# A head's two keys projected with the pairs, kept raw in DRAM, and prepared beside its queries

## The chip, the cores and the metric

The kernel runs on one core of a Trainium2 chip. The metric is the device time of one execution in microseconds (us); the time before is the median of three runs, 2295.79 us (2294.99 to 2299.85).

## The reference, cut to what matters

One step of a two-layer trunk over 512 latent ("sample") and 128 context ("prompt") tokens, 640 columns here. The odd layer projects its normed input with one matrix and splits the columns; mixer C is differential attention over four heads, each with two queries, two keys and a value of twice the width.

```python
cq, ck, cv, cg, dq, dk, dv, dg = split_cols(h @ w_in, ODD_SPLIT)
cq, ck = rms_norm(cq, cqn), rms_norm(ck, ckn)        # per head, 128 wide
# sample tokens: rope on cq and ck; cached context keys and values joined ahead
o1 = attend(cq[:, 0], ck_all[:, 0], cv_all)
o2 = attend(cq[:, 1], ck_all[:, 1], cv_all)
o_c = rms_norm(o1 - lam * o2, c_on) * (1.0 - lam_init)
y_c = o_c * silu(cg)
```

The prompt tokens' normed keys are an output too (`new_c_k`).

## The kernel before, in words

Activations lie transposed, features on partitions, in 16 tiles `h` of 128 x 640, each as a high and a low fp32r part; products are formed from three matmuls (high x high, high x low, low x high). A tile of 128 output columns is made from 16 weight blocks. The weights come in quarters of four blocks (256 KB, `load_raw`, on SP's queue), which ACT and VectorE split into `wh` and `wl` (lines 220 and 221, four buffers each); a quarter is 24 matmuls, two halves of 320 columns.

The odd projection has four stages.

1. Six gate tiles (`FRONT[:6]`), projected directly.
2. `run_pairs` (line 444): the rest of `FRONT`, 16 tiles of values and gates, two at a time. A pair is computed as one 2 x 2 block product in seven products of 24 matmuls (`Q1 N5 P6 Q2 P7 Q3 P4`, lines 535 to 537) from sums of weight halves, which VectorE makes, and sums of `h` halves, made before. The two results go to `kept` tiles (lines 1384 to 1399) and to DRAM on POOL's queue (line 1362): values raw to `vdram`, gates to `ydram`. During N5 the first halves of `h[0..7]` hold other data; behind the last pair's P7 they are read back from `hdram` (line 1404).
3. `run_tiles` (line 317, called at 1570) with attention beside it. The first three jobs, query 0, query 1 and key 0 of head 3, are **leads**: they go through the weights together, quarter by quarter, with three PSUM pairs. Then one tile per job, each quarter's matmuls followed by `slot()` (line 308), which advances every generator in `prep` by one step; `proj_parts` advances attention five times per tile. The leads' preparations are begun one behind the other during and right behind job 3 (`settle`, line 378).
4. The output projection.

Preparing a key (`k_gen`, line 578): the projected tile is staged in SBUF, transposed to rows on TensorE (`to_rows`, line 560: four 128 x 128 blocks of the sample and one of the prompt, each group into one of the two PSUM buffers `T`), squared and summed on ACT (line 589, five squares), multiplied by the gain on VectorE (591, 594), scaled by the root from POOL (596 to 598), rotated (605 to 609), and, some steps later, transposed back and split into `k0h`, `k0l` (613 to 622). The context's cached key goes the same way through `ctxk`. Preparing a query (`q_gen`, 627): `qx` and `qsq` on ACT (631, 632), four copies `qsw` (635), three VectorE operations (636 to 639), then sums of squares by TensorE into a `T` buffer (643) and transposes of those (651). The values are read from `vdram` (`v_load`, 693) and laid out by `v_kept` (698), which puts the head's attention into `attn`. `scores` (741), `soft` (712) and `diff_gen` (1437) are the attention.

A scheduler fixes each engine's order when the program is built; every engine then runs its list in order.

Of the kernel before, what the change touches and what calls it, by code (L numbers as in the profile page):

```python
# [11 lines left out]
F32 = mybir.dt.float32  # L12
# [8 lines left out]
P = 128  # L21
# [4 lines left out]
NT = NS + NP  # L26
# [14 lines left out]
P_BUFS = 4  # L41
# [9 lines left out]
def trunk_kernel(ctx: ExitStack, tc: tile.TileContext, I: dict, O: dict):  # L51
    nc = tc.nc
# [17 lines left out]
    pools = {}  # L70
# [212 lines left out]

    prep, attn = [], []

# [31 lines left out]
    def run_tiles(jobs, w_ap, make_h, fill=None, rate=0.0, ahead=None, order=(0, 1, 2, 3), before=None,  # L317
                  last=None, by_half=False, mid=False, trans=[], grace=0, cut=None, summed=None, led=None, freed=None):
# [13 lines left out]
        units = [(pos, qd, js) for pos, qd in enumerate(order) for js in (cut or [(0, 4)])]  # L332
        for ui, (pos, qd, js) in enumerate(units):
# [64 lines left out]
        t = 0  # L398
        if before:
            settle()  # L400
        else:
            n = pending.pop(0)
            begin(jobs[n][1], pps[n])
# [173 lines left out]

    def k_gen(ap, pp, tag, src, gain, new_out, then=None, more=0):
# [20 lines left out]
        nc.gpsimd.dma_start(new_out, kg[:, 4, :])  # L599
        m1 = ap.tile([P, 4, P], F32, tag="rp", name="m1", bufs=3)  # L600
        m2 = ap.tile([P, 4, P], F32, tag="rp", name="m2", bufs=3)
        x = kg[:, 0:4, :].rearrange("p b (a h f) -> p (b a) h f", a=2, h=2)
# [244 lines left out]
    xdram = [dram.tile([P, NT], F32, name=f"xd{k}") for k in range(KT)]  # L847
    vdram = [dram.tile([P, NT], F32, name=f"vd{k}") for k in range(10)]
    hdram = [dram.tile([P, 2, HALF], F32R, name=f"hd{k}") for k in range(8)]

# [480 lines left out]
    def forms1():  # L1331
# [3 lines left out]
        for j, tag in enumerate((3, 4, 5, 6, 7, 1, 2, 0)):  # L1335
# [7 lines left out]
            if j in (4, 6):  # L1343
# [9 lines left out]
    def front_col(kind, i):  # L1353
        return (OD["cv"] + i * P if i < 8 else OD["dv"] + (i - 8) * P) if kind == "v" else \
            (OD["cg"] + i * P if i < 8 else OD["dg"] + (i - 8) * P)
# [4 lines left out]
    def keep_tile(n):  # L1360
        kind, i = FRONT[n]
        nc.gpsimd.dma_start((vdram if kind == "v" else ydram)[i], st["kept", n])

# [188 lines left out]
    heads = (3, 0, 1, 2)  # L1552
    for n, h in enumerate(heads):
        load, vgen = v_then(256, I["cache_c_v"][0, 0, h], (2 * h, 2 * h + 1), O["new_c_v"][0, 0, h], diff_then(n, h))
        for m in range(2):
            jobs.append((OD["cq"] + (m * 4 + h) * P, q_job(f"q{m}" + "ab"[n % 2], "c_q_norm")))
        for m in range(2):
            job = k_job(f"k{m}", I["cache_c_k"][0, 0, m, h], "c_k_norm", O["new_c_k"][0, 0, m, h], *((vgen, 1 - min(n, 1)) if m else (None, 1)))
            jobs.append((OD["ck"] + (m * 4 + h) * P, job if m else with_load(load, job)))
# [110 lines left out]
```

## Time and profile before

| | |
|---|---|
| median of three runs | 2295.79 us |
| the profiled execution | 2294.4 us, span 2292.6 us |
| TensorE busy | 2255.9 us |
| VectorE, ACT, POOL busy | 1589.8, 1088.9, 160.0 us |
| pairs ahead of attention | 1220.8 to 1417.8 us |
| first plain matmul behind them | 1417.8 us |
| granted TensorE clock | 0.999 |

The busy time of an engine is the union of its instructions' times. Matmuls overlap by design of the record, so the pace of TensorE is read from the distance between starts. A gap on TensorE has its own mark in the timeline: the idle time in brackets and what ended it.

### The profile page before, as it was taken

How to read it: one execution, taken by the hardware profiler on the slowest of the kernel's cores; microseconds unless marked ns; L12 is line 12 of the kernel's file. 1: busy time of each engine (PE TensorE's matmuls, PEld its weight loads, DVE VectorE, ACT ScalarE, POOL GpSimd, SP SyncE). 2: the span in 40 equal slices, each digit the busy share in tenths (PEclk: the TensorE clock that was granted, in tenths of full speed). 3: DMA queues.
4: the chain of work that ended last, by engine and by line, in shares of the span. 5: the costliest groups of instructions: out<-in, count | busy, mean ns of one | idle time of the engine just before them, and what ended most of it. 6: DMA issues, size and time to landing. Idle time of an engine off the chain costs nothing.

```text
span 2292.6 us, 41100 instructions
## 1 busy us (share of the span) xinstructions
PE 2255.9 (98%) x15900; PEld 2178.0 (95%) x15900; DVE 1589.8 (69%) x2831; ACT 1088.9 (47%) x2304; POOL 160.0 (7%) x224
## 2 busy tenths in 40 slices
PE   7999999999999999999999999999999999999999
PEld 5889999999999999999999999999999999999999
DVE  4666968779779776887787665365665655557775
ACT  5325652443522222544464443465565676755443
POOL 1001000000000000000100001011111100000101
PEclk9999999999999999999999999999999999999999
DMA  9985537547367564854553335223223221238642
GB/s 321 294 270 161 158 113 218 152 133 219 116 210 216 177 191 137 277 173 140 164 155 108 116 118 152 79 60 104 79 63 101 71 60 49 76 101 269 184 138 62
DMA packets 380899, 342.89 MB, mean 150 GB/s; under 512 B 16402, under 2 KB 338416, under 8 KB 380192
## 3 DMA queue, kind: packets, MB, share of 16 engines
q1 hardware_dynamic: 366288, 296.00, 43.0%
q0 software_dynamic: 13696, 42.10, 5.4%
q8 instruction: 125, 2.05, 0.4%
q10 hardware_dynamic: 720, 2.16, 0.3%
q14 instruction: 70, 0.57, 0.1%
HBM read 301.27 MB, written 38.93 MB: 148 GB/s over the span
## 4 chain that ended last, share of the span: by engine, by line
PE 85%; DVE 4%; ACT 4%; DMA 3%; issue 3%; POOL 1%; SPq 0%; ACTq 0%; POOLq 0%; DVEq 0%
PE pq L537 7%; PE pq L536 7%; PE pq L535 7%; PE pa L256 6%; PE pa L257 6%; PE pb L256 6%; PE pa L258 6%; PE pb L257 6%; PE pb L258 6%; PE pb L271 2%; PE pb L270 2%; PE pa L270 2%; PE pb L272 2%; PE pa L272 2%; PE pa L271 2%
## 5 line engine op out<-in xcount | busy, mean ns | idle before, releaser
L220 ACT ACTIVATE wh<-raw 128x512 fp32r<-128x512 f32 (+1 forms) x456 | 273.1, 600 | 574.0 <-PE pb L257 406.9
L221 DVE TENSOR_TENSOR wl<-raw,wh 128x512 fp32r<-128x512 f32 (+1 forms) x456 | 295.7, 650 | 212.3 <-ACT wh L220 191.9
L256 PE MATMUL pa<-h,wh 128*128 128x320 f32 x1024 | 325.3, 319 | 4.3 <-ACT h L220 2.0
L257 PE MATMUL pa<-h,wh 128*128 128x320 f32 x1024 | 319.5, 313 | 1.7 <-DVE h L221 0.8
L258 PE MATMUL pa<-h,wl 128*128 128x320 f32 x1024 | 318.2, 311 | 0.9 <-DVE wl L221 0.9
L257 PE MATMUL pb<-h,wh 128*128 128x320 f32 x1024 | 317.1, 310 | 0.0
L258 PE MATMUL pb<-h,wl 128*128 128x320 f32 x1024 | 316.8, 309 | 0.0
L256 PE MATMUL pb<-h,wh 128*128 128x320 f32 x1024 | 316.6, 310 | 0.0
L198 DVE SCALAR_TENSOR_TENSOR acc<-adaw,sT,acc 128x1024 f32<-128x1024 f32 x240 | 299.7, 1276 | 0.0
L256 PEld LDWEIGHTS pa<-h,wh 128*128 128x128 f32 x1024 | 193.1, 189 | 18.3 <-issue 10.0
L257 PEld LDWEIGHTS pa<-h,wh 128*128 128x128 f32 x1024 | 193.3, 189 | 7.6 <-issue 3.3
L535 PE MATMUL pq<-h,wh 128*128 128x320 f32 x640 | 198.7, 311 | 0.4 <-ACT wh L220 0.4
L537 PE MATMUL pq<-h,wl 128*128 128x320 f32 x640 | 198.0, 309 | 0.1
L536 PE MATMUL pq<-h,wh 128*128 128x320 f32 x640 | 197.7, 309 | 0.0
L258 PEld LDWEIGHTS pa<-h,wl 128*128 128x128 f32 x1024 | 193.1, 189 | 3.5 <-issue 2.1
L257 PEld LDWEIGHTS pb<-h,wh 128*128 128x128 f32 x1024 | 192.2, 188 | 1.0 <-issue 0.8
L256 PEld LDWEIGHTS pb<-h,wh 128*128 128x128 f32 x1024 | 192.1, 188 | 0.8 <-issue 0.4
L258 PEld LDWEIGHTS pb<-h,wl 128*128 128x128 f32 x1024 | 192.3, 188 | 0.0
L537 PE MATMUL pq<-T,wl 128*128 128x320 f32 x480 | 147.7, 308 | 0.2 <-DVE wl L221 0.2
L536 PE MATMUL pq<-T,wh 128*128 128x320 f32 x480 | 147.9, 308 | 0.0
L535 PE MATMUL pq<-T,wh 128*128 128x320 f32 x480 | 147.6, 308 | 0.1
L270 PE MATMUL pa<-h,wh 128*128 128x320 f32 x432 | 141.0, 326 | 0.0
(431 smaller groups left out, 5306.0 us busy)
## 6 DMA issues: line engine op xcount, KB each, us to landing
adaw<-in_ada_w SPq DMA_DIRECT2D x128, 512.0 KB, 4.3
raw<-in_ev_w_in SPq DMA_DIRECT2D x176, 256.0 KB, 3.5
raw<-in_od_w_in SPq DMA_DIRECT2D x160, 256.0 KB, 2.9
ada<-in_ada_w SPq DMA_DIRECT2D x32, 1024.0 KB, 7.9
w<-in_od_w_in SPq DMA_DIRECT2D x24, 512.0 KB, 4.0
yd<-y POOLq DMA_DIRECT2D x32, 320.0 KB, 3.2
yin<-yd SPq DMA_DIRECT2D x32, 320.0 KB, 4.5
w<-yd SPq DMA_DIRECT2D x32, 320.0 KB, 4.2
```

What stands on the lines that cost most here:

```text
L198: V.scalar_tensor_tensor(out=acc[c], in0=w, scalar=sT[:, kt, c:c + 1], in1=acc[c], op0=ALU.mult, op1=ALU.add)
L220: A.activation(hi, x, AF.Copy)
L221: V.tensor_sub(lo, x, hi)
L256: PE.matmul(ps, wh[:, i, :], hi[:, sl], start=(j == js[0] if alone else (pos == 0 and j == 0)), stop=False)
L257: PE.matmul(ps, wh[:, i, :], lo[:, sl], start=False, stop=False)
L258: last_mm[0] = PE.matmul(ps, wl[:, i, :], hi[:, sl], start=False, stop=(j == js[1] - 1 if alone else (pos == 3 and j == 3)))
L270: PE.matmul(ps, wh[:, j, :], hi[:, sl], start=(qd == 0 and j == 0), stop=False)
L271: PE.matmul(ps, wh[:, j, :], lo[:, sl], start=False, stop=False)
L272: PE.matmul(ps, wl[:, j, :], hi[:, sl], start=False, stop=(qd == 3 and j == 3))
L535: PE.matmul(ps, wh[:, j, :], hi, start=(new and h == 0 and j == 0), stop=False, **kw)
L536: PE.matmul(ps, wh[:, j, :], lo, start=False, stop=False, **kw)
L537: PE.matmul(ps, wl[:, j, :], hi, start=False, stop=(h == 1 and j == 3), **kw)
```

## The change

The two keys of head 3, the first differential head, are taken out of the jobs of stage 3 and put into `FRONT` as a ninth pair, tiles of kind `"r"`, behind the other heads' values and ahead of the last four value tiles. Like values they are kept raw, and go to two DRAM tiles `rdram`. `run_tiles` is called without leads (`n_lead=0`): query 0 and query 1 of head 3 are now plain jobs 0 and 1. Ahead of it `odd_start()` (the constants of the layer) and `first_head()` are called: the latter loads both raw keys into two of the attention's four `P` buffers, the value tile and its context, and puts a generator into a new list `early`, advanced once per `slot()` ahead of `prep`. After two idle steps it runs key 0's `k_gen`, key 1's and then the values' `v_kept`. These `k_gen`s read the raw tile where others stage theirs, and have their row tiles in the buffer of the value tile `vh` (`places`) instead of the three `rp` buffers.

```diff
     def slot(fill=None, rate=0.0, attend=True):
+        advance(early, len(early))
         advance(prep, len(prep))
...
-            leads, held, lp = list(range(min(3, len(jobs)))), [], None
+            leads, held, lp = list(range(n_lead)), [], None
...
-        x = stage(ap, pp)
+        x = stage(ap, pp) if places is None else pp
         yield
         ss = small.tile([P, 5], F32, tag="ss", name="ss")
-        kg = ap.tile([P, 5, P], F32, tag="rp", name="kg", bufs=3)
+        kg = place(0, 5, "kg")
...
-                                                for t in (("v", a), ("v", a + 1), ("g", b), ("g", b + 1))] +         [("v", i) for i in (4, 5, 8, 9)]
+                                                for t in (("v", a), ("v", a + 1), ("g", b), ("g", b + 1))] + \
+        [("r", i) for i in range(2)] + [("v", i) for i in (4, 5, 8, 9)]
...
+    FIRST = [OD["ck"] + (m * 4 + 3) * P for m in range(2)]
...
+    def first_head():
+
+        ap = pools["cur"]
+        raws = []
+        for i in range(2):
+            raws.append(ap.tile([P, 768], F32, tag="P", name="first", bufs=P_BUFS)[:, 0:NT])
+            nc.sync.dma_start(raws[-1], rdram[i])
+        load, vgen = c_then(0)
+        load()
+
+        def keys():
+            yield
+            yield
+            for m, x in enumerate(raws):
+                tag, src, gain, new_out = k_args(m, heads[0])
+                yield from k_gen(ap, x, tag, src, gains[gain], new_out, more=1,
+                                 places=ap.tile([P, 14, P], F32, tag="vh", name="kpl"))
+            yield from vgen()
+
+        early.append(keys())
...
-    run_tiles(jobs, I["od_w_in"][0], lambda k: odd_start() if k == 8 else None, mid=True)
+    odd_start()
+    first_head()
+    run_tiles(jobs, I["od_w_in"][0], None, mid=True, n_lead=0)
```

How the built program's rows stand now. On ACT, the first place is where key 0 of head 3 is squared. Before (`stg` is the staged key, `junk,ss` a square with its sum, `wh` a weight split):

```order
L646 COPY qs<-T 96x256
L557 COPY stg<-pa 128x320
L220 ACTIVATE wh<-raw 128x512
L557 COPY stg<-pb 128x320
L589 ACTIVATE junk,ss<-T 128x128 x5
L220 ACTIVATE k0h<-T 128x256
```

After (line 596 is the square, 637 `qx`, 638 `qsq` and 641 `qsw` of the first query):

```order
L220 ACTIVATE wh<-raw 128x512
L637 ACTIVATE qx<-pb,vec 128x320
L596 ACTIVATE junk,ss<-T 128x128
L638 ACTIVATE qsq<-pb 128x320
L596 ACTIVATE junk,ss<-T 128x128
L641 COPY qsw<-qx 32x512
L596 ACTIVATE junk,ss<-T 128x128
L641 COPY qsw<-qx 32x512
L596 ACTIVATE junk,ss<-T 128x128
L641 COPY qsw<-qx 32x512
L596 ACTIVATE junk,ss<-T 128x128
L641 COPY qsw<-qx 32x512
```

The staging copies are gone, and the five squares, which stood in one row, alternate with the first query's work. Key 1 and the second query stand in the same way.

On VectorE, at the same place, before (`kg` the gained and normed rows, `m` the rotated ones, `k0l` a split of the laid-out key):

```order
L591 TENSOR_TENSOR kg<-T,gain_rows 128x512
L594 TENSOR_TENSOR kg<-T,gain_rows 128x128
L596 TENSOR_SCALAR ss<-ss 128x5
L598 TENSOR_TENSOR kg<-kg,r 128x640
L221 TENSOR_TENSOR k0l<-T,k0h 128x256
L605 TENSOR_TENSOR m_16631<-kg,tables 128x512
L606 SCALAR_TENSOR_TENSOR m_16632<-kg,tables 128x8x32
L608 TENSOR_TENSOR m_16632<-kg,tables 128x8x32
L221 TENSOR_TENSOR wl<-raw,wh 128x512
L609 TENSOR_TENSOR m_16631<-m_16631,m_16632 128x512
```

After (`kpl` are the rows in the value's buffer, `qsw` and `qm` the query's):

```order
L598 TENSOR_TENSOR kpl<-T,gain_rows 128x512
L601 TENSOR_TENSOR kpl<-T,gain_rows 128x128
L603 TENSOR_SCALAR ss<-ss 128x5
L642 TENSOR_TENSOR qsw<-qsw,tables 128x512
L605 TENSOR_TENSOR kpl<-kpl,r 128x640
L645 TENSOR_TENSOR qm<-qm,qsw 128x512
L611 TENSOR_TENSOR kpl<-kpl,tables 128x512
L612 SCALAR_TENSOR_TENSOR kpl<-kpl,tables 128x8x32
L614 TENSOR_TENSOR kpl<-kpl,tables 128x8x32
L221 TENSOR_TENSOR wl<-raw,wh 128x512
L615 TENSOR_TENSOR kpl<-kpl 128x512
```

Two operations of the query have come into the key's chain, and the context's split has left it.

On SP's queue, behind the pairs' last weights, before:

```order
L233 DMA raw<-in_od_w_in 128x4x128 x8
L1415 DMA lam_16213<-in_c_lambda 128x512
L1427 DMA con<-in_c_out_norm 128x256
L233 DMA raw<-in_od_w_in 128x4x128
L695 DMA vraw<-vd_194 128x640
L669 DMA ctxv<-in_cache_c_v 128x2x256
L580 DMA ctxk<-in_cache_c_k 128x2x128
```

After (`first` are the raw keys):

```order
L233 DMA raw<-in_od_w_in 128x4x128 x8
L1427 DMA lam_16268<-in_c_lambda 128x512
L1439 DMA con<-in_c_out_norm 128x256
L1579 DMA first<-rd_198 128x640
L1579 DMA first<-rd_199 128x640
L701 DMA vraw<-vd_194 128x640
L675 DMA ctxv<-in_cache_c_v 128x2x256
L587 DMA ctxk<-in_cache_c_k 128x2x128
```

The two raw keys stand behind the constants, and one weight load has moved behind the whole group; the eight weight loads ahead are now the two query tiles' own.

On TensorE, counted in quarters of 24 plain matmuls from the last pair: key 0's first transposes stand behind 4 quarters, the first query's sums of squares (L649) 25 matmuls behind them, key 0's layout behind 7, key 1's two places behind 8 and 11, the value tiles' transposes 4 matmuls behind key 1's layout and 20 matmuls behind that, and the first scores behind 12.9. Before, the first scores stood behind 20.9. TensorE's list is 24 instructions shorter, all of them projection matmuls. From shortly behind the first scores, every engine's list is that of before.

More of the change, by code (lines that the diff above doesn't have):

```diff
@@ L331, in run_tiles @@
                else new_pp(1 + held.index(n) if trans else n) for n in leads}
-        units = [(pos, qd, js) for pos, qd in enumerate(order) for js in (cut or [(0, 4)])]
+        units = [(pos, qd, js) for pos, qd in enumerate(order) for js in (cut or [(0, 4)])] if leads else []
         for ui, (pos, qd, js) in enumerate(units):
@@ L400, in run_tiles @@
             settle()
-        else:
+        elif pending:
             n = pending.pop(0)
@@ L575, in gate, with k_gen, place @@
                                    op0=ALU.add, op1=ALU.mult)
-    def k_gen(ap, pp, tag, src, gain, new_out, then=None, more=0):
+    def k_gen(ap, pp, tag, src, gain, new_out, then=None, more=0, places=None):
+        def place(c, b, name):
+            if places is None:
+                return ap.tile([P, b, P], F32, tag="rp", name=name, bufs=3)
+            return places[:, c:c + b, :]
         raw = ap.tile([P, 2, P], F32, tag="ctxk", name="ctxk", bufs=1)
         nc.sync.dma_start(raw, src.rearrange("(c p) d -> p c d", p=P))
-        x = stage(ap, pp)
+        x = stage(ap, pp) if places is None else pp
         yield
         ss = small.tile([P, 5], F32, tag="ss", name="ss")
-        kg = ap.tile([P, 5, P], F32, tag="rp", name="kg", bufs=3)
+        kg = place(0, 5, "kg")
         junk = ap.tile([P, P], F32, tag="junk", name="junk", bufs=1)
@@ L848, in trunk_kernel @@
     vdram = [dram.tile([P, NT], F32, name=f"vd{k}") for k in range(10)]
+    rdram = [dram.tile([P, NT], F32, name=f"rd{k}") for k in range(2)]
     hdram = [dram.tile([P, 2, HALF], F32R, name=f"hd{k}") for k in range(8)]
@@ L1361, in keep_tile @@
         kind, i = FRONT[n]
-        nc.gpsimd.dma_start((vdram if kind == "v" else ydram)[i], st["kept", n])
+        nc.gpsimd.dma_start({"v": vdram, "g": ydram, "r": rdram}[kind][i], st["kept", n])
     def gate_of(dst, src, sign=1):
@@ L1552, in trunk_kernel, with k_args, c_then @@
     heads = (3, 0, 1, 2)
[L1553 to L1554 removed]
+    def k_args(m, h):
+        return f"k{m}", I["cache_c_k"][0, 0, m, h], "c_k_norm", O["new_c_k"][0, 0, m, h]
+    def c_then(n):
+        h = heads[n]
+        return v_then(256, I["cache_c_v"][0, 0, h], (2 * h, 2 * h + 1), O["new_c_v"][0, 0, h], diff_then(n, h))
+    def first_head():
[15 more added lines that the diff above has]
+        early.append(keys())
+    for m in range(2):
+        jobs.append((OD["cq"] + (m * 4 + heads[0]) * P, q_job(f"q{m}a", "c_q_norm")))
+    for n in range(1, 4):
+        h = heads[n]
+        load, vgen = c_then(n)
         for m in range(2):
```

12 lines of the change are left out of this document (7 added, 5 removed).

## The prediction

> **What bounds the kernel now.** I read the page first: which engine is full, and what the chain that ended last is made of.
>
> ```profile
> span 2292.6 us, 41100 instructions
> PE 2255.9 (98%) x15900; PEld 2178.0 (95%) x15900; DVE 1589.8 (69%) x2831; ACT 1088.9 (47%) x2304; POOL 160.0 (7%) x224
> PE 85%; DVE 4%; ACT 4%; DMA 3%; issue 3%; POOL 1%; SPq 0%; ACTq 0%; POOLq 0%; DVEq 0%
> ```
>
> TensorE is busy 98% of the span and makes up 85% of the chain: time goes away if TensorE gets fewer instructions or waits less, and in no other way. The execution took 2294.4 us, 1.8 us more than its span and 1.4 us under the median of the runs, 2295.79 us. The change touches the stretch from the last pairs to the first scores of attention, so I next cut that stretch into windows of 20 us (the columns are PE busy time with instructions, granted clock, DMA share, GB/s).
>
> ```profile
> 1400.00:1420.00 20.00, 20.00 (x138) 1.00 0.78 207
> 1440.00:1460.00 20.00, 20.00 (x138) 1.00 0.23 68
> 1460.00:1480.00 20.00, 19.87 (x141) 1.00 0.28 79
> 1480.00:1500.00 20.00, 18.38 (x129) 1.00 0.30 82
> 1500.00:1520.00 20.00, 19.80 (x137) 1.00 0.23 71
> ```
>
> TensorE has no gap through the pairs and the three leads, at full clock; it loses about 2 us between 1460 and 1520, where the first head is prepared. So there are two things to price: the matmuls, and these gaps.
>
> **The matmuls.** The busy time of one matmul (0.31) overlaps with its neighbours, so I take the distance of starts. The TensorE timeline gives the first pair's first matmul, the last pair's last, and the first of the leads:
>
> ```profile
> 1220.83 0.31 PE L535 MATMUL pq<-h,wh 128*128 128x320 f32 x1
> ...
> 1417.65 0.31 PE L537 MATMUL pq<-T,wl 128*128 128x320 f32 x1
> 1417.79 0.31 PE L256 MATMUL pb<-h,wh 128*128 128x320 f32 x1
> ```
>
> Eight pairs of 7 products of 24 matmuls are 1344, in 1417.79 - 1220.83 = 196.96 us: **0.1466 us each**, without a gap. Two plain tiles are 2 x 96 = 192 matmuls, a pair is 168. The change turns two plain tiles into a pair: 24 matmuls fewer, 24 x 0.1466 = **-3.52 us**. Everything else that TensorE does for the head (transposes, sums of squares, scores) stays, in number and size. The extra pair's VectorE and ACT work (operand sums, splits, two kept tiles) lies under gapless matmuls as that of the eight pairs does; without that cover a pair's last sums into its tiles would show, two of them:
>
> ```profile
> L1396 DVE TENSOR_TENSOR kept<-pq,tables x10: 490/491/492, 1235.1 to 1414.5; 128x320 f32<-128x320 f32 x10
> ```
>
> 2 x 0.49 = 1.0 us.
>
> The Trainium skill ("TensorE: Matmul & The Clock Gate", Back-to-back issue gap and the table ahead of it) has the warm distance as the columns over 2.4 GHz plus 2.5 ns. For 320 columns that is an estimate of 0.136 us and would make this term 3.26 us; the rows above say 0.1466, and they are used.
>
> **The waits that go.** In the stretch with gaps the timeline shows where starts are farther apart than the work:
>
> ```profile
> 1478.76 0.31 PE L272 MATMUL pb<-h,wl 128*128 128x320 f32 x1
> 1479.21 0.44 PE L617 MATMUL T<-ident,ctxk 128*128 128x128 f32 x2
> ...
> 1483.29 0.31 PE L272 MATMUL pb<-h,wl 128*128 128x320 f32 x1
> 1484.46 0.66 PE L564 MATMUL T<-ident,m 128*128 128x128 f32 x4 [0.86 <-DVE m L609]
> ...
> 1486.53 0.77 PE L564 MATMUL T<-ident,stg 128*128 128x128 f32 x5
> 1487.05 0.39 PE L271 MATMUL pa<-h,wh 128*128 128x320 f32 x1
> ...
> 1493.59 0.38 PE L617 MATMUL T<-ident,ctxk 128*128 128x128 f32 x2
> 1494.73 0.66 PE L564 MATMUL T<-ident,m 128*128 128x128 f32 x4 [0.77 <-DVE m L609]
> ...
> 1500.72 0.30 PE L272 MATMUL pa<-h,wl 128*128 128x320 f32 x1
> 1501.23 0.74 PE L564 MATMUL T<-ident,vraw 128*128 128x128 f32 x5 [0.20 <-DMA vraw<-vd]
> ```
>
> Less 0.147 for the matmul ahead (0.17 for the two context transposes at 1493.59), TensorE stood 0.30, 1.02, 0.97 and 0.36 us: **2.65 us**. The two long ones are the keys' rotated rows `m`: the transposes that read them come 8.2 us behind those that began the chain (1486.53 to 1494.73), because after the leads both queries and both keys are prepared one behind the other in little TensorE time. In the changed order, key 0 is transposed after 4 quarters (24 matmuls each) of the first query tile, and its `m1` is wanted after 7; key 1 stands at 8 and 11. Three quarters are 72 x 0.1466 = 10.6 us, plus some 1.3 us of transposes and sums between: 11.9 us. These waits go.
>
> **The waits that come.** In front.md ACT's rows show the change's own price: the squares of a key no longer stand five in a row but alternate with the query's copies. What these cost, on ACT, and who takes the transposed key afterwards:
>
> ```profile
> 1453.18 0.63 ACT L220 ACTIVATE wh<-raw 128x512 fp32r<-128x512 f32 x1 [0.76 <-PE pb L257]
> 1453.72 0.51 ACT L631 ACTIVATE qx<-pb,vec 128x320 f32<-128x320 f32 x1
> 1454.13 0.43 ACT L632 ACTIVATE qsq<-pb 128x320 f32<-128x320 f32 x1
> 1454.58 2.51 ACT L635 COPY qsw<-qx 32x512 f32<-32x512 f32 x4
> ...
> 1487.30 0.28 ACT L589 ACTIVATE junk<-T 128x128 f32<-128x128 f32 x1 [0.68 <-PE T L564]
> ...
> 1488.50 0.28 ACT L589 ACTIVATE junk<-T 128x128 f32<-128x128 f32 x1
> ```
>
> ```profile
> 1488.90 0.69 DVE L591 TENSOR_TENSOR kg<-T,gain_rows 128x512 f32<-128x512 f32 x1 [1.55 <-ACT junk L589]
> ```
>
> By distance of starts a square is (1488.50 - 1487.30) / 3 = 0.40, a weight split 0.54, `qx` 0.41, `qsq` 0.45, a `qsw` copy 0.63; VectorE's gain product starts 0.40 behind the start of the fourth square and takes 0.69. Count from the key's first transpose: the weight split starts at about 0.1 (its buffer comes free with the quarter's end), `qx` at 0.6, the first square at 1.0; then square, `qsq`, square, `qsw`, square, `qsw` = 1.2 + 0.45 + 1.26 = 2.9, so the fourth square starts at 3.9, the product at 4.3, and the PSUM buffer is free at 5.0. There are two such buffers; the second holds the prompt's block, and the query's sums of squares (L643) want the first. TensorE comes to them after the five transposes (1486.53 to 1487.05: 0.5) and 25 matmuls (3.66), at 4.2: **a wait of 0.8 us**, for each key: 1.6. Behind these sums TensorE's whole projection is queued, since it runs in order. The bounds: nothing if the product did not wait for the squares; 1.7 for each if the fifth square and its copies counted too.
>
> On that wait the Trainium skill ("PSUM — Partial Sum Buffer", PSUM bank collisions raise a hardware error) says that ScalarE and VectorE may not even read one bank at once, so that software keeps them apart. The 1.55 us that VectorE waited for the last square in the row above agrees. By that rule the term is 1.6 us as worked out; were the two readers free of each other, the buffer would be free with the fourth square at 4.3, and the term 0.2 us.
>
> Smaller ones. When a key is laid out, its third transpose group waits for the split of the first, which stands behind a weight split on both engines:
>
> ```profile
> 1494.17 0.37 ACT L220 ACTIVATE k1h<-T 128x256 fp32r<-128x256 f32 x1
> ```
>
> ```profile
> 1494.59 0.69 DVE L221 TENSOR_TENSOR wl<-raw,wh 128x512 fp32r<-128x512 f32 x1
> 1495.19 0.42 DVE L221 TENSOR_TENSOR k1l<-T,k1h 128x256 fp32r<-128x256 f32 x1
> ```
>
> With VectorE's weight split at 0.7 behind the first transpose, the key's split ends at 0.7 + 0.6 + 0.42 = 1.7, plus 0.1 until TensorE starts; TensorE arrives after six transposes and 7 matmuls, at 0.6 + 1.03 = 1.6: 0.15 for each key, 0.3 (bounds 0 and 1.0). The second value tile is loaded when the first is transposed:
>
> ```profile
> 1498.13 4.21 SPq L695 DMA_DIRECT2D vraw<-vd  x2
> ```
>
> From this issue to the transposes at 1501.23 it took 3.1 us. In the changed order 20 matmuls (2.93) stand there: 0.2 (bounds 0 and 1.9, its slowest landing of 4.8 in place of 2.9). The second scores come 19 matmuls and the sums behind the first, and wait for the first ones' exponential; 0.2, between 0 and the 0.9 of the longest such wait in the list of waits:
>
> ```profile
> PE S L747 <- ACT p L721: 1.5, 4, 0.9
> DMA to landing us min/median/max: 2.8/2.9/4.8
> ```
>
> New waits: 1.6 + 0.3 + 0.2 + 0.2 = **2.3 us** (all bounds at once: 0, and 7.2).
>
> **What is moved and costs nothing.** SP sends the constants, two raw keys, the value tile, and both contexts behind the eighth weight load, as it sent them before without the keys; the next weights are wanted 28 us later. The key loads have the room from the last pair's end to quarter 4, 14.1 us. The reload of the saved halves of `h`, which the first plain tile now needs 3.5 us sooner, is over before the pairs end in any case:
>
> ```profile
> L1404 POOL DMA_DIRECT2D h<-hd x8: 696/707/737, 1397.6 to 1402.5; - x8
> DMA to landing us min/median/max: 3.4/5.3/6.1
> ```
>
> 1402.5 + 6.1 = 1408.6, and the first user starts at 1417.79. From the third tile of queries on, every engine's instructions stand in the order of before, so I carry nothing on from there.
>
> **Sum.** -3.52 - 2.65 + 2.3 = **-3.9 us**. On the profiled execution's 2294.4 that is 2290.5; on the median of the runs, 2295.79, it is **2291.9 us**, which I forecast. 0.2%, about what a measurement of this kernel can tell from no change, is 4.6 us: the forecast lies just inside, on the faster side.
>
> **Rivals.**
> *The new waits stay small.* If ACT's order costs TensorE little (each term near its lower bound, 0.6 in all), -3.52 - 2.65 + 0.6 = -5.6: 2290.2 us, faster by 0.24%. For it: the estimate of the squares' wait is a difference of two sums of seven terms, 5.0 and 4.2, and half a microsecond in either is easily had. Against: each term was read from starts, queueing included.
> *The rotated rows are late again.* The key's chain was 8.2 us. The fourth square comes 1.9 us later in it than behind an undivided row of squares (3.9 against 0.8 + 1.2), and two of the query's VectorE operations now stand in it, of the weight split's size (0.6 by its distance to the next row above): 11.3 us, against 11.9. Missing that by 1.5 for each key costs 3 us: -0.9, 2294.9 us, no change that can be told.
> *The raw keys come late* (the slower side). They are loaded behind the constants, which wait for the pairs' memory:
>
> ```profile
> 1419.65 0.50 SPq L1415 DMA_DIRECT2D lam<-in_c_lambda  x1
> ...
> L1427 SPq DMA_DIRECT2D con<-in_c_out_norm x1: 452/452/452, 1420.2 to 1420.2; - x1
> DMA to landing us min/median/max: 6.4/6.4/6.4
> ```
>
> Issued at about 1421.2 and 1421.7 on that clock and landing in 6.4, they are there at 1428, 4 us before quarter 4 at 1431.9. Past that TensorE stands one for one, and slower by over 0.2% takes a landing of 6.4 + 4 + 3.9 + 4.6 = 19 us, as three of the slowest landings shown here in a row: 2301 us.
>
> A gap that long could cost the clock too: the Trainium skill ("TensorE: Matmul & The Clock Gate", Part 1: The HAM clock gate) halves it after an idle window of about 3.4 us. The gaps of 1 us quoted above left it at 1.00; no row of this stretch shows a longer one.
>
> **How the numbers follow.** Forecast 0.59; small waits 0.31; late rows 0.06; late keys 0.04. The first rival alone is over the 0.2%: faster 0.31, slower 0.04, the rest 0.65. The range takes in the first two rivals and the 1.4 us between the profiled execution and the median: 2289.0 to 2295.5; with all upper bounds at once it would be 2296.8, which I leave out with the late keys.
>
> **What would show it.** Right: nine pairs of 24.6 us; key transposes named `first`; TensorE waits of about 0.8 us ahead of L649 at its first two queries, released by VectorE's gain product (L598); no wait for the rows of L615. Wrong: a wait for the DMA of `first`; a wait at L615; or gaps from the third query tile on that were not there before.

## The result, and the profile after

The changed kernel takes **2291.94 us** in the median of 12 runs (2286.91 to 2298.80), beside 2295.00 us for the kernel before (12 runs, 2293.32 to 2300.08). The ratio is 0.9979, 95% interval 0.9970 to 0.9989: 4.8 us faster, 2.5 to 6.9 (the two medians alone lie 3.1 us apart). The forecast was 2291.9 us. In a second measurement, below, the ratio was 0.9987 (0.9977 to 0.9996).

The profiled execution happens to be the longest of its 12 runs, 2298.8 us, though the part of the program that was changed is shorter in it; where the rest came from is told at the end of this section. Its page:

```profile
span 2297.0 us, 41082 instructions
...
PE 2257.0 (98%) x15876; PEld 2179.4 (95%) x15876; DVE 1600.2 (70%) x2845; ACT 1093.0 (48%) x2311; POOL 163.4 (7%) x226
...
PE 87%; ACT 4%; DVE 4%; DMA 3%; issue 1%; POOL 0%; SPq 0%; ACTq 0%; DVEq 0%; POOLq 0%
```

TensorE has 24 instructions fewer (15876 against 15900) and is as full as before. So the whole span says little, and I compare one stretch: from the first pair's first matmul to fixed later starts. The timeline of TensorE after:

```profile
1226.84 0.31 PE L537 MATMUL pq<-h,wh 128*128 128x320 f32 x1
...
1448.27 0.31 PE L539 MATMUL pq<-T,wl 128*128 128x320 f32 x1
1448.42 0.31 PE L270 MATMUL pa<-h,wh 128*128 128x320 f32 x1
...
1586.77 0.34 PE L753 MATMUL S<-k0h,q0bh 128*128 128x384 f32 x1
```

and the same scores (the second head's first) before:

```profile
1585.29 0.34 PE L747 MATMUL S<-k0h,q0bh 128*128 128x384 f32 x1
```

Nine pairs take 1448.42 - 1226.84 = 221.58 us, 24.62 each, as eight took 24.62 each. From the first pair to the second head's first scores it is 1586.77 - 1226.84 = **359.9 us**, against 1585.29 - 1220.83 = 364.5: 4.5 us less. The windows of the stretch, and a late one (columns as in the prediction):

```profile
1440.00:1460.00 20.00, 20.00 (x138) 1.00 0.79 251
1460.00:1480.00 20.00, 19.59 (x141) 1.00 0.32 93
1480.00:1500.00 20.00, 19.54 (x138) 1.00 0.33 99
1500.00:1520.00 20.00, 19.86 (x136) 1.00 0.23 71
2080.00:2100.00 20.00, 17.74 (x95) 0.83 0.67 215
```

Between 1460 and 1520 TensorE now loses 1.0 us, where it lost about 2. In the list of waits between 1440 and 1640 one line is left of it:

```profile
PE T L649 <- DVE kpl L598: 0.8, 2, 0.4
```

The rotated rows (`m`, now `kpl`) are gone from it, and the forecast's own new wait has come: VectorE's gain product releases the query's sums, twice.

What made the execution long lies outside the stretch. Its first pair starts 6.0 us later than before's, ahead of everything that was changed, and from the last scores of attention to the last projection's first pairs it takes 76.6 us instead of 73.1. The last window above stands in that second place: at 0.83 of the clock, and with gaps, TensorE issued 95 matmuls in 20 us, where before it issued 134 at 1.00 in the same window. Such falls of the granted clock stand outside the changed stretch: in this execution at 960 (0.91), 1120 (0.94), 1140 (0.89) and 2080 us, in that of before only at 1120 (0.83), apart from the last 10 us of either. The runs of one kernel spread over 4 to 12 us with them. I therefore give two things for each experiment: the stretch on TensorE, which repeats within 0.6 us, and the ratio of whole runs, which is good to about 0.1%.

### The profile page after: what moved, and what is told of

Its sections match the earlier page's. It is cut to its first block, busy times and chain, and to the rows that moved or that the text cites. A ratio compares the mean times of both kernels' runs of the same rounds, so it can differ in the third digit from the quotient of the medians.

```text
span 2297.0 us, 41082 instructions
## 1 busy us (share of the span) xinstructions
PE 2257.0 (98%) x15876; PEld 2179.4 (95%) x15876; DVE 1600.2 (70%) x2845; ACT 1093.0 (48%) x2311; POOL 163.4 (7%) x226
## 4 chain that ended last, share of the span: by engine, by line
PE 87%; ACT 4%; DVE 4%; DMA 3%; issue 1%; POOL 0%; SPq 0%; ACTq 0%; DVEq 0%; POOLq 0%
PE pq L539 7%; PE pq L538 7%; PE pq L537 7%; PE pa L256 6%; PE pa L257 6%; PE pa L258 6%; PE pb L256 6%; PE pb L257 6%; PE pb L258 6%; PE pb L271 2%; PE pb L270 2%; PE pb L272 2%; PE pa L270 2%; PE pa L272 2%; PE pa L271 2%; PE T L741 2%
## 5 line engine op out<-in xcount | busy, mean ns | idle before, releaser
L256 PE MATMUL pa<-h,wh 128*128 128x320 f32 x992 | 316.2, 320 | 7.7 <-ACT h L220 4.1
L257 PE MATMUL pa<-h,wh 128*128 128x320 f32 x992 | 310.9, 314 | 2.8 <-DVE h L221 1.6
L258 PE MATMUL pa<-h,wl 128*128 128x320 f32 x992 | 309.3, 312 | 0.0
L257 PE MATMUL pb<-h,wh 128*128 128x320 f32 x992 | 308.1, 311 | 0.0
L258 PE MATMUL pb<-h,wl 128*128 128x320 f32 x992 | 307.9, 310 | 0.0
L256 PE MATMUL pb<-h,wh 128*128 128x320 f32 x992 | 307.5, 311 | 0.0
L256 PEld LDWEIGHTS pa<-h,wh 128*128 128x128 f32 x992 | 187.9, 190 | 21.9 <-issue 10.1
L537 PE MATMUL pq<-h,wh 128*128 128x320 f32 x672 | 208.6, 310 | 0.0
L539 PE MATMUL pq<-h,wl 128*128 128x320 f32 x672 | 207.9, 309 | 0.1
L538 PE MATMUL pq<-h,wh 128*128 128x320 f32 x672 | 207.6, 309 | 0.0
L257 PEld LDWEIGHTS pa<-h,wh 128*128 128x128 f32 x992 | 188.3, 190 | 9.0 <-DVE h L221 3.9
L257 PEld LDWEIGHTS pb<-h,wh 128*128 128x128 f32 x992 | 186.9, 188 | 1.0 <-issue 0.8
L256 PEld LDWEIGHTS pb<-h,wh 128*128 128x128 f32 x992 | 186.8, 188 | 0.9 <-issue 0.4
L539 PE MATMUL pq<-T,wl 128*128 128x320 f32 x504 | 155.1, 308 | 0.2 <-DVE wl L221 0.2
L538 PE MATMUL pq<-T,wh 128*128 128x320 f32 x504 | 155.3, 308 | 0.0
L537 PE MATMUL pq<-T,wh 128*128 128x320 f32 x504 | 155.0, 308 | 0.1
L270 PE MATMUL pa<-h,wh 128*128 128x320 f32 x448 | 146.0, 326 | 0.0
```

Source lines behind the costliest of these rows:

```text
L256: PE.matmul(ps, wh[:, i, :], hi[:, sl], start=(j == js[0] if alone else (pos == 0 and j == 0)), stop=False)
L257: PE.matmul(ps, wh[:, i, :], lo[:, sl], start=False, stop=False)
L258: last_mm[0] = PE.matmul(ps, wl[:, i, :], hi[:, sl], start=False, stop=(j == js[1] - 1 if alone else (pos == 3 and j == 3)))
L270: PE.matmul(ps, wh[:, j, :], hi[:, sl], start=(qd == 0 and j == 0), stop=False)
L537: PE.matmul(ps, wh[:, j, :], hi, start=(new and h == 0 and j == 0), stop=False, **kw)
L538: PE.matmul(ps, wh[:, j, :], lo, start=False, stop=False, **kw)
```

## The experiments

The stretch runs from the first pair's first matmul to the first scores `S<-k1h,q0bh`, near 2013 us, late in the third stage; it is 792.3 us before. In `line_alone`, 28.15 us are added for the two tiles ahead of the pairs (192 x 0.1466).

| run | stretch, against before | ratio to before (95%) |
|---|---|---|
| the change | -4.8 | 0.9979 (0.9970 to 0.9989) |
| `change_again` | -4.2 | 0.9987 (0.9977 to 0.9996) |
| `line_alone` | +0.1 | 0.9981 (0.9971 to 0.9990) |
| `two_leads` | -0.3 | 1.0005 (0.9994 to 1.0015) |
| `no_leads` | -1.8 | 0.9987 (0.9977 to 0.9997) |
| `step_earlier` | -4.1 | 0.9987 (0.9976 to 0.9998) |
| `copied_first` | -4.1 | 0.9984 (0.9975 to 0.9993) |
| `earlier_held` | -5.7 | 0.9995 (0.9985 to 1.0004) |
| `held_again` | -5.8 | 0.9981 (0.9972 to 0.9990) |
| `no_idle_steps` | -0.4 | one run |
| `step_later` | -2.9 | one run |
| `parity_back` | -4.1 | 0.9977 (0.9967 to 0.9988) |
| `parity_flip` | +2.0 | 1.0010 (0.9999 to 1.0022) |

### The line without the pair: `line_alone`

```diff
-    FRONT = [("g", i) for i in range(10, 16)] + [t for a, b in ((6, 0), (0, 2), (2, 4))
+    FRONT = [("g", i) for i in range(10, 13)] + [("r", i) for i in range(2)] + [("g", i) for i in range(13, 16)] + [t for a, b in ((6, 0), (0, 2), (2, 4))
...
-        [("r", i) for i in range(2)] + [("v", i) for i in (4, 5, 8, 9)]
-    N_FRONT = 6
+        [("v", i) for i in (4, 5, 8, 9)]
+    N_FRONT = 8
...
```

> The keys' early line without the pair: both keys are two plain tiles of 96 matmuls ahead of the pairs, kept raw in DRAM, and then prepared beside the query tiles as in the change. If the terms are additive as forecast (pair -3.5 us; waits -2.65 that go and about +1.9 that come), TensorE has the matmuls of the kernel before (192 for the two keys), eight pairs, and the stretch from the first kept plain tile to the first scores of attention is 3.5 us longer than with the change and 0.8 us shorter than before: about 2294 us against 2295. The waits ahead of L649 (0.57 each) and the missing waits for the rotated rows stay as in the change. Rival, the pair is all of it (the waits that come cost as much as those that go): no difference to before. Rival, the line is all of it and the pair's matmuls are eaten by something else: as fast as the change, 4 to 5 us under before.

The waits ahead of L649 are the change's. But the stretch is as long as before, not 0.8 us shorter: the second value tile came late.

```profile
PE T L566 <- DMA vraw<-vd: 1.2, 2, 1.0
PE T L649 <- DVE kpl L598: 0.8, 2, 0.4
```

By the distance of starts TensorE stood 1.15 us for that tile, where it stood 0.21 in the change's profile. Without those 0.94 us the line alone is -0.9, as forecast. So most of the gain in the stretch is the pair's matmuls. The whole runs came out faster than that (-4.4 us, 2.3 to 6.7), as fast as the change: by them alone the last rival, that the line is all of it, would stand, and only the stretch speaks against it. Their mean granted clock was 0.9985 against 0.9980 of before, by estimate 1.1 us, and behind the stretch the profile is 1.0 us shorter than before's (last section of the experiments); the rest stays open.

### Leads and line: `two_leads`, `no_leads`

In the change, and in the kernel before (where `n_lead` also becomes a parameter of `run_tiles`):

```diff
-    run_tiles(jobs, I["od_w_in"][0], None, mid=True, n_lead=0)
+    run_tiles(jobs, I["od_w_in"][0], lambda k: None, mid=True, n_lead=2)
```

```diff
...
-    run_tiles(jobs, I["od_w_in"][0], lambda k: odd_start() if k == 8 else None, mid=True)
+    odd_start()
+    run_tiles(jobs, I["od_w_in"][0], None, mid=True, n_lead=0)
```

> The change, but the two query tiles lead together again (quarter by quarter, sharing h) in place of one behind the other, so the keys' line starts two tiles later, beside the second head's queries. If what costs is that queries and keys are prepared in one heap, nothing comes back: the stretch from the first pair to the first scores stays within 1 us of the change, with waits ahead of L649 of 0.5 us each at new places and none of 1 us for the rotated rows. Rival, tiles that lead together are themselves what makes the gaps (their copies to staging, the late value tile): 1 to 2 us of gaps come back, and the stretch is 1 to 2 us longer than with the change.

> The kernel before, with the first three tiles no longer led together: both queries and both keys are plain tiles one behind the other, no pair, no raw keys, no early line. Theory: the waits of 1.02 and 0.97 us for the rotated rows were made by preparing queries and keys in one heap after the leads, so most of the 2.65 us of waits goes here too, and TensorE keeps its 24 matmuls: 1.5 to 2.7 us under before in the stretch from the first pair to the first scores, so 2293 us against 2295, and no wait longer than 0.6 us at L564. Rival, the rotated rows are late wherever the two keys stand behind their own projections: the waits at L564 for m stay at 0.8 to 1.0 us each, and the time is that of before.

With two leads the pair's 3.52 us are saved and nearly all of it is lost again. To the second head's scores it is 0.8 us behind the change, but the waits go on behind them, and at the end of the stretch it is 4.5 us behind (waits between 1440 and 1640):

```profile
PE T L1500 <- DVE on L1494: 1.2, 2, 0.7
PE T L566 <- DVE m L615: 0.7, 1, 0.7
PE T L649 <- DVE kpl L598: 0.4, 1, 0.4
PE T L657 <- DVE kpl L598: 0.4, 1, 0.4
...
```

Neither expectation was right. The keys' line, two tiles later, delays attention by 30 us (its first scores come at 304.8 us of the stretch instead of 274.1), so the first head's output (`on`) and the second head's rotated rows (`m`) now fall on VectorE together. A heap had been moved, not taken apart.

`no_leads` keeps the plain tiles and has one wait left of 0.2 us or more up to the second head:

```profile
PE T L565 <- DMA vraw<-vd: 0.3, 1, 0.3
```

The 1.02 and 0.97 us for the rotated rows are gone without pair or early line: they were the leads' doing. (The leads' preparations are begun in the loop over the tiles, one whenever `prep` is empty; `settle` is not called in this stage.) 1.8 us of the 2.65 are had by this alone.

### The wait at L649: `step_earlier`, `copied_first`, `step_later`

One idle `yield` of `keys()` fewer; the transposed key copied to SBUF ahead of its squares; one `yield` more:

```diff
         def keys():
             yield
-            yield
```

```diff
             t = to_rows(cols_of(x), sample)
+            if places is not None:
+                rows = kg[:, 0:4, :] if sample else kg[:, 4:5, :]
+                V.tensor_copy(rows, t.rearrange("p (b f) -> p b f", b=4 if sample else 1))
+                t = rows.rearrange("p b f -> p (b f)")
```

```diff
             yield
             yield
+            yield
```

> The change with one idle step fewer ahead of the keys' line: each key's transposes stand one quarter of a query tile (24 matmuls, 3.5 us) earlier, so its squares no longer alternate with the query's scale, square and copies, and the sums of L649 come more than one quarter behind the transposes. Theory (the wait of 0.57 us at L649 is the first PSUM buffer held by the gain product behind squares that stand among the query's copies): both waits at L649 go, 1.1 us in all; the raw keys, which were there 3.0 us ahead of their transposes, are wanted 3.5 us earlier, so up to 0.5 us is lost ahead of the first transposes. Together 0.6 to 1.1 us shorter than the change from the first pair to the first scores. Rival, the buffer is held as long for another reason (the squares' own length): the wait moves to the next user of that buffer and the stretch stays as it was.

> The change, with the transposed key copied out of PSUM by VectorE before it is squared; the squares and the gain product then read the copy, and the PSUM buffer is free after the copy. Everything stands where it stood. Theory (the 0.57 us at L649 are the PSUM buffer, held by the gain product behind the squares): both waits go, 1.1 us; VectorE has some 0.9 us more in each key's chain, against 1.9 us of slack ahead of the rotated rows' transposes, so nothing comes back there: from the first pair to the second head's first scores about 358.8 us against 359.9 of the change. Rival (VectorE and ACT are simply behind at that place, among weight splits and the query's operations): the wait stays, or a wait of that size for a weight split comes in its place, 359.9 or more.

> One idle step more: the key's transposes stand one quarter later, behind the query's scale, square and copies on ACT instead of among them, but L649 follows only 21 matmuls (3.1 us) behind them. Theory A (the wait is the alternation on ACT): an undivided row of squares ends sooner, the buffer is free about 3.2 us after the transposes and the wait at L649 is under 0.3 us each; 358.9 us plus what later attention costs. Theory B (the buffer is held some 4.7 us whatever stands between): 1.0 us or more at each L649, 360.8 us.

The waits of `step_earlier` and of `copied_first`, from 1410 to 1600:

```profile
PE T L657 <- DVE ptl L221: 0.9, 1, 0.9
PE S L753 <- ACT p L727: 0.4, 1, 0.4
PE T L566 <- DMA vraw<-vd: 0.2, 1, 0.2
PE T L566 <- DVE m L615: 0.2, 1, 0.2
```

```profile
PE T L566 <- DMA vraw<-vd: 0.9, 2, 0.8
```

In both, L649 (L653 in the second) waits no more. `copied_first` leaves TensorE's order as it was but for two instructions, so the cause is shown: the PSUM buffer, held until the gain product has read it behind the squares. Both theories had the run shorter than the change, and neither was. In `copied_first` that is due to the value tile again (0.96 us against 0.21) and some 0.1 us at four places of the keys' layout, which the added copies delay. `step_earlier` gave back the 0.9 and 0.4 us of its list; that this is because the values came a quarter earlier too, so that attention met the queries' work at another place, is what `earlier_held` tests below.

`step_later` fits neither theory: 0.61 and 0.63 us, between "under 0.3" and "1.0 or more". Its squares do stand closer, and the product follows (ACT, then VectorE):

```profile
1462.83 0.26 ACT L596 ACTIVATE junk<-T 128x128 f32<-128x128 f32 x1
...
1464.40 0.27 ACT L596 ACTIVATE junk<-T 128x128 f32<-128x128 f32 x1
```

```profile
1464.53 0.69 DVE L221 TENSOR_TENSOR q0al<-qm,q0ah 128x512 fp32r<-128x512 f32 x1 [0.33 <-ACT q0ah L220]
1465.14 0.68 DVE L598 TENSOR_TENSOR kpl<-T,gain_rows 128x512 f32<-128x512 f32 x1
```

Four squares start within 1.6 us, where they took 2.6 in the change; the product starts 3.5 us behind the transposes (1461.64) instead of 4.0, and would have started up to 0.3 us sooner but for VectorE's split ahead of it. So the alternation's share of the hold is 0.5 to 0.9 us; the rest is weight split, squares and product, whatever stands between. Its stretch is longer than the change's all the same, for a third L649 waits 1.0 us for a split of attention weights.

### What a late raw key costs: `no_idle_steps`

```diff
         def keys():
-            yield
-            yield
             for m, x in enumerate(raws):
...
+            yield
+            yield
             yield from vgen()
```

> Both idle steps stand behind the keys, ahead of the value tiles: the first key's transposes come 54 matmuls (7.9 us) behind the last pair in place of 96 (14.1). The raw keys were there some 11 us behind the last pair. Theory (TensorE stands one for one for late raw keys): about 3 us of wait ahead of the first transposes, by the DMA of first; the waits at L649 go (1.1 us), since the squares are past by then: about 361.8 us from the first pair to the second head's first scores, against 359.9. Rival (the loads land sooner than they are seen to be used): no wait, 358.7 us.

The wait was there, 2.88 us between starts less 0.15, but the stretch grew by more: 364.3 us to the second head's scores instead of 361.8.

```profile
1451.46 0.31 PE L272 MATMUL pa<-h,wl 128*128 128x320 f32 x1
1454.34 0.74 PE L566 MATMUL T<-ident,first 128*128 128x128 f32 x5 [2.57 <-DMA first<-rd]
...
1455.42 0.47 PE L270 MATMUL pa<-h,wh 128*128 128x320 f32 x1
1455.69 0.47 PE L271 MATMUL pa<-h,wh 128*128 128x320 f32 x1
```

Behind the gap the matmuls start 0.267 us apart, until 1458.8, and only then 0.147 again: 13 matmuls at 0.12 more are 1.6 us; the granted clock is 0.66 between 1455 and 1460, and 1.00 in the change's profile there. The rest are two waits of 0.5 us for the split ahead of the keys' third transposes. So this gap on TensorE was not paid one for one.

### A better place: `earlier_held`, `change_again`, `held_again`

`step_earlier` with the idle step put ahead of the values, measured twice; `change_again` is the change as it stands, beside the second of these:

```diff
         def keys():
             yield
-            yield
             for m, x in enumerate(raws):
...
+            yield
             yield from vgen()
```

> The key's transposes one quarter of a tile earlier, as in the run before with one idle step fewer, but the idle step is put ahead of the value tiles, so that these and the first scores stand where the change has them. Theory: the waits at L649 (0.57 each) go as they went there, and what that run gave back (0.4 us for the exponential at its third scores, 1.0 us ahead of the transposes of L657 behind a split of the attention weights) goes too, since attention meets the query tiles where it did in the change: 358.7 us from the first pair to the second head's first scores against 359.9, and about 5.9 us under before. Rival (what was given back is due to keys that end earlier, not to attention's place): 360.5 us as there.

> The changed kernel once more, on the same chip as the next run. If the places where TensorE's clock falls (near 960, 1130 and 2085 us) are chance and not the kernel's, this profile shows others than the first (0.91 at 960, 0.89 at 1140, 0.83 at 2080), and the stretch from the last scores of attention to the end differs from its 232.8 us by some us, while the stretch from the first pair to the second head's first scores is 359.9 us again, within 0.5. The ratio to before: 0.998.

> The kernel with the keys a quarter earlier and the value tiles held, once more beside the change. Locally it was 1.2 us shorter than the change (358.7 against 359.9), yet its runs took 3 us longer in the median, with a mean granted clock of 0.9970 against 0.9978. Theory (the clock falls by chance, outside the stretch): here its median is 1 us under that of the change and its mean clock the same. Rival (what is gained in the stretch lets TensorE run into a wait behind it, at the start of the last projection near 2085 us, that costs the clock): its median is again no better than the change's, its mean clock is lower, and its profile shows the fall at 2080 us again.

To the second head's scores it was 358.7 us, as expected, and 358.9 the second time; the change took 359.9 and 360.4 (the 0.5 are its second value tile, 0.82 us this time). All that is left of the waits, in `earlier_held`:

```profile
PE S L753 <- ACT p L727: 0.2, 1, 0.2
```

In whole runs the first measurement did not show it (2295.11 us); beside the change on the same chip it was 2292.97 us against 2294.20, the 1.2 us of the stretch. Two medians of 11 runs with such a spread are weak evidence for 1.2 us; the stretch is the better one. The falls of the clock differ between the two profiles of one kernel (the change's second has none at 960 and 2080). Part of the rival holds all the same: both profiles of the held kernel have a fall at 2080, and its mean clock was again lower, 0.9975 against 0.9979. Over all the profiles this one fall goes with the kernel: of the nine runs with the pair and the change's turn of buffers (next section) seven have it, all but `change_again` and `copied_first`; of the five others none has. Chance alone is therefore a poor account of it, though no run was made to separate the two.

### Behind the stretch: `parity_back`, `parity_flip`

Comparing starts at the end of the third stage showed an effect of the change that the prediction does not have. Before, the last projection's first matmul waited for the last gate:

```profile
2070.62 0.31 PE L272 MATMUL pb<-h,wl 128*128 128x320 f32 x1
2072.57 0.42 PE L256 MATMUL pa<-h,wh 128*128 128x320 f32 x1 [1.64 <-DVE gg L1004]
```

Plain tiles take two PSUM buffers in turn, `(i - lead) % 2`. With two jobs and three leads fewer, the last tile has the other buffer, and that wait is gone. One line puts the turn back in the change, or gives the change's turn to before:

```diff
-            pp = new_pp((i - lead) % 2)
+            pp = new_pp((i - lead + mid) % 2)
```

> The change, with the query, key and value tiles' two PSUM buffers taken in the other turn, so that the last tile again stands in the buffer that the next projection's first tile wants, as before the change. Ahead of the last projection the change's profile has TensorE going on at once (11.9 us from the last scores to its first matmul), before's has a wait of 1.64 us for the last gate's product (13.7). Theory: the gain there is only lent: the reloaded tiles yin are sent 19.9 us behind the last scores in both, and TensorE waits for them where it came sooner; so 13.7 us again with one wait of 1.6 us, shorter waits for h behind it, and the first pairs of that projection begin no later than the change's, 75 to 76.6 us behind the last scores; the total is that of the change within 1 us. Rival: the 1.8 us are a real part of the gain, and the total is 1.8 us over the change's.

> The kernel before with nothing but that turn of the two PSUM buffers changed, as the change leaves it. Theory (the wait of 1.64 us for the last gate's product only moves to the reloaded tiles): the first matmul of the last projection comes 11.9 us behind the last scores in place of 13.7, TensorE waits up to 1.8 us for h behind it, and its first pairs begin 73 us behind the last scores as before: no difference in the total within 1 us. Rival: the turn is a gain of its own that the change brought along, 1.8 us under before in the stretch behind the last scores, and 71.3 us to the first pairs.

With the turn put back the wait is there again (1.15 us), and the first pairs of the last projection come 73.1 us behind the last scores of attention, against 76.6 and 75.0 in the change's two profiles and 73.1 before. So the change has not gained the 1.8 us. The tiles that the last projection reads back (`yin`) are the limit there, and without the one wait TensorE has several, in the change's first profile:

```profile
2083.62 0.42 PE L256 MATMUL pa<-h,wh 128*128 128x320 f32 x1 [0.41 <-ACT h L220]
2084.48 0.41 PE L257 MATMUL pa<-h,wh 128*128 128x320 f32 x1 [0.44 <-DVE h L221]
...
2086.94 0.63 PE L256 MATMUL pa<-h,wh 128*128 128x320 f32 x1 [0.89 <-ACT h L220]
2087.80 0.63 PE L257 MATMUL pa<-h,wh 128*128 128x320 f32 x1 [0.23 <-DVE h L221]
```

and with the turn back:

```profile
2070.64 0.41 PE L256 MATMUL pa<-h,wh 128*128 128x320 f32 x1 [1.15 <-DVE gg L1011]
2082.43 0.42 PE L257 MATMUL pa<-h,wh 128*128 128x320 f32 x1 [0.38 <-DVE h L221]
```

The turn itself is no loss, however. `line_alone` and `no_leads` have the change's turn too, go on without the wait, and begin the last projection's first pairs 72.1 and 71.9 us behind the last scores, a microsecond sooner than before. Their next `yin` loads are sent from 18.8 and 18.6 us behind the last scores on, against 19.9 in the change's two profiles, and neither has a fall of the clock there. Why the tiles go out later in the change stays open.

`parity_flip` begins these pairs at 73.6 us, as the theory had it, but loses 1.9 us at the other end, which nothing had foreseen: the first tile behind the leads now wants a buffer that a lead still holds. ACT squares that lead's query out of a `pa` until 1468.16, and the first tile's matmuls come behind it, with a wait for an earlier copy on ACT ahead of them:

```profile
1467.73 0.43 ACT L632 ACTIVATE qsq<-pa 128x320 f32<-128x320 f32 x1
```

```profile
1467.88 0.38 PE L651 MATMUL T<-ident,qs 96*128 96x96 f32 x2 [1.64 <-ACT qs L646]
1468.22 0.41 PE L270 MATMUL pa<-h,wh 128*128 128x320 f32 x1
```

Whole runs do not separate `parity_back` (0.9977) from the change. Its profile has no fall of the clock at 2080, and the mean clock of its runs was 0.9984, against 0.9978 and 0.9979 of the change's.

## Why the prediction was right

**The matmuls, -3.52 us.** Measured: nine pairs at the pace of eight, without a gap, and 24 matmuls fewer. The cover held.

**The waits that go, -2.65 us.** All four went. `no_leads` shows that the two long ones came from the leads' heap, as argued.

**The waits that come, +2.3 us.** By distance of starts less 0.147 they are, in the change's first profile, 0.57 and 0.58 ahead of L649 (0.8 each forecast), 0.12 twice at the key's layout (0.15), 0.21 for the second value tile (0.2) and 0.30 for the second scores (0.2): 1.9 us. The rows behind the largest, on ACT, VectorE and TensorE:

```profile
1463.50 0.27 ACT L596 ACTIVATE junk<-T 128x128 f32<-128x128 f32 x1
...
1464.07 0.29 ACT L596 ACTIVATE junk<-T 128x128 f32<-128x128 f32 x1
...
1464.99 0.26 ACT L596 ACTIVATE junk<-T 128x128 f32<-128x128 f32 x1
...
1466.14 0.28 ACT L596 ACTIVATE junk<-T 128x128 f32<-128x128 f32 x1
```

```profile
1466.54 0.69 DVE L598 TENSOR_TENSOR kpl<-T,gain_rows 128x512 f32<-128x512 f32 x1 [2.03 <-ACT junk L596]
```

```profile
1462.50 0.71 PE L566 MATMUL T<-ident,first 128*128 128x128 f32 x5
...
1466.56 0.31 PE L270 MATMUL pa<-h,wh 128*128 128x320 f32 x1
1467.28 0.63 PE L649 MATMUL T<-qsq,ones 128*32 128x256 f32 x6 [0.41 <-DVE kpl L598]
```

From the first transpose (1462.50) the fourth square came 3.64 us later (3.9 forecast), the product 4.04 (4.3), and TensorE was free for the sums at 4.21 (4.2). The working was off by 0.26 us in a sum of seven terms, and that is the whole error of this term. The second value tile is the loose one: 0.21, 0.82, 1.15, 0.96 and 0.71 us in the five profiles in which it stands 20 matmuls behind its issue (the change twice, `line_alone`, `copied_first`, `parity_back`). That the first profile met the forecast 0.2 is luck.

**The sum.** -3.52 - 2.65 + 1.9 = -4.3, against -4.5 measured to the second head's scores. In the second profile the new waits are 2.4, and -3.7 stands against -4.1. Forecast -3.9. So the terms account for the stretch within 0.4 us. That the median of the whole runs, 2291.94 us, met the forecast within 0.1 us is luck: its runs spread over 12 us, and the interval of the gain is 2.5 to 6.9 us, 0.9 to 5.3 in the second measurement. Two bounds of the prediction are added up a little wrong, which changes nothing: 2290.2 less 1.4 is 2288.8, not 2289.0, and the upper bound of the wait at L649 comes to 1.8 us by its own terms, not 1.7.

**"I carry nothing on from there."** The instructions' order is the same, but their buffers are not: the turn of the two PSUM buffers moved a wait at the end. The step was incomplete, and by the prediction's own sign (gaps from the third query tile on that were not there before) this part of it was wrong. Against `parity_back`, the change's two profiles lose 1.9 and 3.5 us behind the stretch, in the second figure with a fall of the clock; whole runs are too wide to confirm that.

**The rivals.** The rotated rows were ready 10.85 us behind the transposes (11.3 estimated) with 1.9 us to spare; the raw keys landed 3.0 us ahead (4 estimated):

```profile
L1579 SPq DMA_DIRECT2D first<-rd x2: 477/502/526, 1451.4 to 1451.9; - x2
...
DMA to landing us min/median/max: 7.3/7.5/7.6
```

1451.9 + 7.6 = 1459.5, and TensorE wants them at 1462.5. "Past that TensorE stands one for one" was wrong: `no_idle_steps` paid 1.6 us more for the clock. The rival of small new waits was not borne out: 1.9 and 2.4 in the two profiles, against its 0.6 and the forecast's 2.3.

## What to carry to other kernels

Work taken off a full engine counts at that engine's own pace, and a preparation moved beside it counts by the waits that it takes and brings, term by term: here -2.65 and +1.9, so that one slow DMA landing cancels it. Preparations piled in one place cost nearly as much as the matmuls saved when two tiles led together here; spread them, and hold back what starts the next stage. When jobs are taken from a list, look also at what is taken in turn by their number: buffers change hands at both ends of the list.

## What the runs showed of the hardware

The clock fell behind shorter idle time than expected, and behind several short gaps too. One gap of 2.88 us between starts, in `no_idle_steps`, brought the pace from 0.147 to 0.267 us for 3.4 us; one of 1.95 us, before, left it at full speed. In the change's first profile no gap near 2085 us is over 1.2 us, yet five between 2082.9 and 2087.8 went with a fall:

```profile
2085.00:2090.00 5.00, 3.59 (x13) 0.65 0.48 160
2090.00:2095.00 5.00, 5.00 (x26) 0.67 0.62 202
```

Short gaps do not do it each time. Near 2085 us three gaps of 0.64, 0.44 and 0.44 us of idle time, within 4 us, left the clock at 1.00 in `change_again`; three of 0.63, 0.45 and 0.45 us, at nearly the same distances, went with 0.67 between 2085 and 2090 in `no_idle_steps`.

The Trainium skill ("TensorE: Matmul & The Clock Gate", Part 1: The HAM clock gate) halves the clock after an idle window of about 3.4 us. The pace does about halve, and for about that long; but the single idle stretch that did it here was 2.7 us, and in the other place it was split into pieces. Here the measurement decides.
